# Mamba-2 part of a hybrid decoder layer on one core: activations pinned in line, a Ln as bias of the decays' exponents, three small steps moved from ScalarE to VectorE

## The chip, the cores and the metric

The kernel runs on one core of a Trainium2 chip. The metric is the device time of one execution in microseconds (us), lower is better. Engines are named as in the profile: PE (TensorE: matmuls), PEld (its weight loads), DVE (VectorE), ACT (ScalarE), POOL (GpSimd), SP (SyncE, which here issues DMAs only).

## The reference

One decoder layer over 256 tokens of width 2048, float32: a token mixer (an HGRN2 branch and a Mamba-2 branch, each gated and projected, then an output projection), cross-attention into 256 memory tokens, a gated feed-forward layer, and a final norm. What matters here is the Mamba-2 branch, cut to its core:

```python
xbc = silu(causal_dwconv(xbc_raw, conv_w, conv_b))      # 4 taps, per channel
xs, bm, cm = split(xbc)                                 # 8 groups of 4 heads of 64; 8 x 128; 8 x 128
dt = softplus(dt_raw + dt_bias);  a = dt * -exp(a_log)
# per group: state-space scan over time with decays exp(cum[t] - cum[s]), t >= s
y = ssd_chunk_scan(xs * dt, a, bm, cm) + d_skip * xs
y = y * silu(z)
y = y * rsqrt(mean(y * y, per group) + eps) * norm_g
```

The kernel computes the scan of a group without chunks: scores `bm^T cm`, multiplied by the decays `exp(cum[t] - cum[s])` and the causal mask, times `xs * dt`.

## The kernel before, in words

**Weights.** All dense products run on PE in a split form: a float32 weight tile of 128x2048 is fetched by SP (`issue`, L147), cast to a rounded high part `hi` on ACT (L133, in two halves of 1024 columns) and its remainder `lo` is formed on DVE (L134). Five buffers each of `hi` and `lo` (WB = 5) hold halves; a cast of a further half waits until PE has finished with the half five before it. `weights()` hands the next tile to PE, and at that point every entry of `background` (generators, one per scan) is advanced by one step. `project` uses one weight tile (two halves, 16 matmuls with `hi`, 16 with `lo`); `project_tok` uses four tiles.

**Order.** The program is written in one order, and a scheduler lays out a fixed instruction list for each engine from it, in which an instruction may be placed earlier if what it needs is there. Matmuls issued within a step are pinned by `keep_in_program_order`: what is pinned keeps its order among all pinned instructions. Each engine runs its list strictly in order. A `tile_critical` block is laid out as one piece.

**The Mamba-2 stage.** For group g, `m2_project(g)` runs four projections; each is joined from PSUM (`join`: a copy on ACT, L266; an add on DVE, L267) and convolved: the tap at lag 0 with the bias on ACT (L714), three further taps on DVE (L717). For even g, `m2_gates` (L701) projects z for two groups. `m2_scan(g)` is a background generator with pauses counted in weight tiles:

- Silu of x (L727), of B and C (L728), and for even g of z (L730); x is turned through DRAM: a DVE transpose (L502), four POOL DMAs out (L505), one back (L733). Eight Relus (L738, L740) form the exponents of the decays in two tiles `e` (lm), and two Exps (L745, L746) make the decays. The first Exp stands in a `tile_critical` block behind an explicit load of the table set `natural_log_exp_and_others` (L744).
- Three tiles later: scores on PE (`misc<-sz`), masked to `a` on DVE (L754) and copied on ACT (L756), multiplied into `e` on DVE (L758, twice); x times dt into `bb` on DVE (L762, twice).
- One tile later: the scan's products on PE (`misc<-e,bb`), then D's skip (L777), and the result is turned (L782).
- Three tiles later: times z (L790), squares with sums (L794, ACT), rsqrt as Ln and Exp (L285, L286, ACT), scaling by it (L798, ACT), and turned again (L801).
- Four tiles later: `split_turned` (L512 scaling on ACT, L281 cast on ACT, L282 remainder on DVE) writes the branch's output in split form.

Group 0's scan is begun by a generator that the last of four gate-and-branch passes of the HGRN2 branch (L811, L822) advances; groups 1 to 7 are projected after that, with z for groups 2, 4 and 6 ahead of those groups.

Of the kernel before, what the change touches and what calls it, by code (L numbers as in the profile page):

```python
# [9 lines left out]
F32 = mybir.dt.float32  # L10
# [3 lines left out]
AF = mybir.ActivationFunctionType  # L14
ALU = mybir.AluOpType
# [4 lines left out]
P = 128  # L20
T = 256
# [20 lines left out]
B = 32  # L42
# [22 lines left out]
def hybrid_trunk(ctx, tc, xT, memT, par, cst, msk, w_k0, w_ka, w_va, w_hg, w_hv, w_hog, w_ghg, w_bhg, w_dt,  # L65
                 w_z, w_m2, w_gm2, w_bm2, w_out, w_q, w_o, w_up, w_dn, fin_g, outT):
    nc = tc.nc
    V, S, G, PE = nc.vector, nc.scalar, nc.gpsimd, nc.tensor
# [20 lines left out]
    for h in range(1, HEADS, 2):  # L89
        order += [w_hg[h - 1 + i // 2, i % 2] for i in range(4)]  # L90
        q = h // 4 + 1
# [224 lines left out]
    ones = cp.tile([P, P], F32, name="ones")  # L316
# [6 lines left out]
    def pc(name, i=0, n=1):  # L323
        o, _ = PCOLS[name]
        return par_t[:, o + i:o + i + n]
# [13 lines left out]
    with tc.tile_pool(name="st", bufs=1) as st:  # L339
# [35 lines left out]
        for kk in range(KD // 2):  # L375
            raw = st.tile([P, 2 * W], F32, name="raw0", bufs=4)
            if kk == 0:
                for k in range(2):
                    nc.sync.dma_start(out=mraw[:, k, :], in_=memT[:, k, :])
                    nc.sync.dma_start(out=raw[:, k * W:(k + 1) * W],  # L380
                                      in_=w_k0[kk, :, k * W:(k + 1) * W])
# [16 lines left out]
        for n in range(KD):  # L398
# [16 lines left out]
            if n >= 10:  # L415
                for k in range((n - 10) * KD // 6, (n - 9) * KD // 6):
                    u = st.tile([P, T], F32, name="u", bufs=2)
                    V.scalar_tensor_tensor(out=u, in0=xraw[:, k, :], scalar=pc("mix_g", k),
                                           in1=r_xb, op0=ALU.mult, op1=ALU.mult)
# [16 lines left out]
                        op0=ALU.mult, op1=ALU.add)  # L436
        V.tensor_scalar(out=lb[:, 2], in0=lb[:, 1], scalar1=1e-30, scalar2=2.0 ** 60,
                        op0=ALU.max, op1=ALU.mult)
# [8 lines left out]
    mp = mx.enter_context(tc.tile_pool(name="mp", bufs=1))  # L447
# [61 lines left out]
    def split_turned(dst, yc, g):  # L509

        y = mp.tile([P, T], F32, name="jt", bufs=2)
        S.activation(out=y.rearrange("p (g b t) -> p g b t", b=P // B, g=2),  # L512
                     in_=yc.rearrange("p (b g t) -> p g b t", b=P // B, g=2), func=AF.Copy, scale=g)
        split(dst, y)
# [128 lines left out]
    for h in range(HEADS):  # L643
        background.append(hg_scan(h, *hg_project(h), vs[h // 4], sgs[h // 4]))
        if h % 2 and h // 4 + 1 == HEADS // 4:

            c = h % 4 // 2
# [56 lines left out]
    def m2_project(g):  # L704
        sz = mp.tile([P, 4, T], F32, name="sz", bufs=2)
        cb = mp.tile([P, 4, T], F32, name="vc", bufs=2)
        nc.sync.dma_start(out=cb, in_=cum_d[4 * g:4 * g + 4, :].partition_broadcast(P))
        for i in range(4):
            c = m2_chunk(g, i)
            ps = project(s2)  # L710
            raw = mp.tile([P, T], F32, name="t", bufs=1)
            join(mp, ps, raw)
            o = sz[:, i, :]
            S.activation(out=o, in_=raw, func=AF.Identity, bias=pc("m2_cb", c),  # L714
                         scale=pc("m2_cw", 4 * c + 3))
            for s in range(1, 4):
                V.scalar_tensor_tensor(out=o[:, s:T], in0=raw[:, 0:T - s],  # L717
                                       scalar=pc("m2_cw", 4 * c + 3 - s), in1=o[:, s:T],
                                       op0=ALU.mult, op1=ALU.add)
        return sz, cb  # L720

    def m2_scan(g, sz, cb, zt):
# [1 line left out]

        xc = mp.tile([P, 2 * T], F32, name="w", bufs=1)
        xv = xc.rearrange("p (m i t) -> p i m t", i=2, t=B)
        S.activation(out=xv, in_=sz[:, 0:2, :].rearrange("p i (m t) -> p i m t", t=B), func=AF.Silu)  # L727
        S.activation(out=sz[:, 2:4, :], in_=sz[:, 2:4, :], func=AF.Silu)  # L728
        if g % 2 == 0:
            S.activation(out=zt, in_=zt, func=AF.Silu)  # L730
        yd = turned(xc, T // B, "x_d")
        x = mp.tile([P, 2, T], F32, name="kq", bufs=2)
        G.dma_start(out=x, in_=yd.rearrange("(q p) c -> p q c", p=P))  # L733
        lm = [mp.tile([P, 2, 3 * P], F32, name=f"e{j}", bufs=1) for j in range(2)]
        for j in range(4):
# [3 lines left out]
                         bias=cum_tok[:, 0, hd:hd + 1])  # L739
            S.activation(out=l[:, T:3 * P], in_=cb[:, j, P:T], func=AF.Relu, scale=-1.0,  # L740
                         bias=cum_tok[:, 1, hd:hd + 1])

        with tc.tile_critical():  # L743
            nc.scalar.preload_act_table_set("natural_log_exp_and_others")  # L744
            S.activation(out=lm[0], in_=lm[0], func=AF.Exp, scale=-1.0)  # L745
        S.activation(out=lm[1], in_=lm[1], func=AF.Exp, scale=-1.0)  # L746
        yield from pause(3)
        bm, cm = sz[:, 2, :], sz[:, 3, :]
        ps = pm_.tile([P, 512], F32, name="misc")
# [5 lines left out]
                        in1=free(tri, 0, [(0, 2), (1, P)]), op=ALU.mult)  # L755
# [5 lines left out]
        for q in range(2):  # L761
            V.tensor_tensor(out=xd[:, q, :].rearrange("p (i b c) -> p i b c", i=2, c=B),  # L762
                            in0=x[:, q, :].rearrange("p (b i c) -> p i b c", i=2, c=B),
                            in1=free(dt_tok, 64 * q + 8 * g, [(4, 2), (1, 4), (0, B)]), op=ALU.mult)
        yield True
        yp = pm_.tile([P, 512], F32, name="misc")
        for j in range(4):
            rows = slice(64 * (j % 2), 64 * (j % 2) + 64)
            o = (j // 2) * T
# [5 lines left out]
        yv = y.rearrange("p (m i t) -> p i m t", i=2, t=B)  # L775
        for i in range(2):
            V.scalar_tensor_tensor(out=yv[:, i], in0=xv[:, i], scalar=pc("m2_d", 2 * g + i),  # L777
                                   in1=yp[:, i * T:(i + 1) * T].rearrange("p (m t) -> p m t", t=B),
                                   op0=ALU.mult, op1=ALU.add)
# [6 lines left out]
        r = mp.tile([P, 4], F32, name="rt", bufs=2)  # L786
        z0 = g % 2 * T
        yv = y.rearrange("p (n q c) -> p q n c", q=2, c=B)
        for q in range(2):
            V.tensor_tensor(  # L790
                out=y.rearrange("p (i b q c) -> p q b i c", i=2, q=2, c=B)[:, q],
                in0=yt[:, q, :].rearrange("p (b i c) -> p b i c", i=2, c=B),
                in1=zt[:, q, z0:z0 + T].rearrange("p (b i c) -> p b i c", i=2, c=B), op=ALU.mult)
            S.activation(out=yt[:, q, :].rearrange("p (n c) -> p n c", c=B), in_=yv[:, q],  # L794
                         func=AF.Square, accum_out=r[:, q:q + 1])
        rsqrt(r[:, 2:4], r[:, 0:2], 1.0 / T, eps2_t)
        for q in range(2):
            S.activation(out=yv[:, q], in_=yv[:, q], func=AF.Copy, scale=r[:, 2 + q:3 + q])  # L798
        yd = turned(y, T // B, "x_d")
        yc = mp.tile([P, 2, T], F32, name="yc", bufs=2)  # L800
        G.dma_start(out=yc, in_=yd.rearrange("(i p) t -> p i t", p=P))  # L801
        yield from pause(4 if g + 1 < GROUPS else 3)
        for i in range(2):
            split_turned(ym[:, 2 * g + i, :], yc[:, i, :], pc("m2_g", 2 * g + i))


    def gate(name="sz"):
# [7 lines left out]
    zt = m2_gates()  # L815
# [317 lines left out]
    def then(ins):  # L1133
        tc.keep_in_program_order(ins)
# [145 lines left out]
```

## Time and profile before

| | |
|---|---|
| median of 3 runs | 2263.75 us (2261.18, 2263.75, 2266.68) |
| profiled execution | 2263.27 us, of which the span 2261.1 us |
| PE busy in the span | 2233.0 us (99%) |
| DVE, ACT busy | 1622.3 us (72%), 1388.9 us (61%) |
| mean granted clock of PE | 0.996 |

The page gives busy time per engine, slices of the span, the chain that ended last, and groups of instructions. A group's row holds its line, engine, operation, tiles out<-in, count, busy us and mean ns of one, and the idle time of the engine just before, with what ended most of it. In a timeline the columns are start us, us, engine, line, operation; a bracket holds the idle time before and its releaser. The Mamba-2 groups 1 to 7 lie at about 720 to 1030 us of the span; PE runs the projections of groups 4 and 5 from 830 to 883 us, z for group 6 to 907 us, and groups 6 and 7 to 965 us.

### The profile page before, as it was taken

Reading aid. Unit: us, or ns where it says so; the run is one execution under the profiler, and the core shown is the slowest. Engines: PE = TensorE matmul, PEld = TensorE weight load, DVE = VectorE, ACT = ScalarE, POOL = GpSimd, SP = SyncE. Lnnn points to the kernel's source line nnn. Section 1 sums busy time; section 2 is a strip of 40 time slices with the busy share of each in tenths; the row PEclk is TensorE's granted clock in tenths of the full one; section 3 lists DMA queues with packets and bytes.
Section 4 is the critical chain, followed back from the end, with each engine's and each line's share of the span. In section 5 each row is a group of like instructions: output and inputs, shape, how many; then the busy total and the mean of one; then the engine's idle time right before and its main releaser. Section 6 shows DMA issues by size and latency. Waiting matters only on the chain.

```text
span 2261.1 us, 33653 instructions
## 1 busy us (share of the span) xinstructions
PE 2233.0 (99%) x13012; PEld 1916.3 (85%) x13012; DVE 1622.3 (72%) x2602; ACT 1388.9 (61%) x2181; POOL 118.1 (5%) x209
## 2 busy tenths in 40 slices
PE   9999999999999999899999999999999999999998
PEld 8888888888888887778888888888888888888887
DVE  8868888886645777665567765677777777779787
ACT  7567677777645687875455654556555555555554
POOL 0000001100100222120000000000000000000000
PEclk9999999999999999999999999999999999999999
DMA  8655555556655666565565644576555555555554
GB/s 311 239 181 181 192 184 180 184 178 217 217 191 197 217 216 209 205 209 200 189 229 210 223 156 175 177 225 215 193 187 189 192 194 190 186 196 214 205 214 158
DMA packets 94495, 453.70 MB, mean 201 GB/s; under 512 B 27744, under 2 KB 32384, under 8 KB 45312
## 3 DMA queue, kind: packets, MB, share of 16 engines
q1 hardware_dynamic: 69600, 432.36, 53.9%
q0 software_dynamic: 7808, 16.79, 2.8%
q10 hardware_dynamic: 16928, 2.42, 0.6%
q8 instruction: 102, 1.67, 0.3%
q14 instruction: 57, 0.47, 0.1%
HBM read 436.81 MB, written 16.81 MB: 201 GB/s over the span
## 4 chain that ended last, share of the span: by engine, by line
PE 56%; ACT 1%; DVE 1%; issue 0%; ACTq 0%; DVEq 0%
PE proj L82 49%; PE misc L82 4%; PE lev L82 3%; DVE lo L134 0%; ACT hi L133 0%; PE lev L844 0%; DVE e L758 0%; ACT L285 0%; ACTq L743 0%; PE lev L924 0%; ACT bb L794 0%; ACT L727 0%; ACT L286 0%; ACT L728 0%; ACT sz L728 0%
## 5 line engine op out<-in xcount | busy, mean ns | idle before, releaser
L134 DVE TENSOR_TENSOR lo<-raw,hi 128x1024 fp32r<-128x1024 f32 x738 | 893.8, 1222 | 471.3 <-ACT hi L133 428.4
L133 ACT CAST hi<-raw 128x1024 fp32r<-128x1024 f32 x737 | 768.5, 1049 | 401.6 <-PE proj L82 374.3
L82 PE MATMUL proj<-s,hi 128*128 128x512 f32 x3440 | 810.7, 391 | 1.4 <-ACT hi L364 1.4
L82 PEld LDWEIGHTS proj<-s,hi 128*128 128x128 f32 x3440 | 638.0, 188 | 129.1 <-ACT hi L364 1.9
L82 PE MATMUL proj<-hi,s 128*128 128x512 f32 x2218 | 695.7, 390 | 1.1 <-ACT hi L133 1.1
L82 PEld LDWEIGHTS proj<-hi,s 128*128 128x128 f32 x2218 | 416.3, 188 | 88.3 <-ACT hi L133 1.7
L82 PEld LDWEIGHTS proj<-s,lo 128*128 128x128 f32 x3440 | 433.3, 192 | 21.4 <-DVE lo L134 5.8
L82 PE MATMUL proj<-s,lo 128*128 128x256 f32 x3440 | 441.1, 284 | 9.2 <-DVE lo L134 9.2
L82 PE MATMUL proj<-lo,s 128*128 128x512 f32 x1109 | 431.8, 389 | 0.8 <-DVE lo L134 0.8
L82 PEld LDWEIGHTS proj<-lo,s 128*128 128x128 f32 x1109 | 208.4, 188 | 43.2 <-DVE lo L134 1.1
L266 ACT COPY jt<-proj 128x256 f32<-128x256 f32 x167 | 61.7, 370 | 84.8 <-PE proj L82 84.7
L168 ACT CAST hi<-raw 128x1024 fp32r<-128x1024 f32 (+1 forms) x56 | 52.1, 944 | 57.0 <-DVE raw L177 30.0
L505 POOL DMA_DIRECT2D x_d<-yq x96 | 55.8, 587 | 314.6 <-DVE yq L502 311.5
L169 DVE TENSOR_TENSOR lo<-raw,hi 128x1024 fp32r<-128x1024 f32 (+1 forms) x56 | 60.4, 1087 | 6.6 <-ACT hi L168 6.0
L717 DVE SCALAR_TENSOR_TENSOR sz<-t,par_t,sz 128x255 f32<-128x255 f32 (+2 forms) x96 | 45.6, 475 | 17.1 <-ACT sz L714 16.1
L505 POOL DMA_DIRECT2D y_d<-yq x64 | 35.0, 553 | 393.6 <-DVE sm L607 286.4
L1011 DVE SCALAR_TENSOR_TENSOR gc<-g,par_t,gc 128x255 f32<-128x255 f32 x88 | 42.2, 480 | 2.0 <-ACT gc L1009 0.6
L82 PE MATMUL proj<-hi,ha 128*128 128x512 f32 x104 | 36.7, 389 | 0.0
L1014 ACT ACTIVATE gc<-gc 128x256 f32<-128x256 f32 x44 | 18.4, 417 | 29.8 <-DVE gc L1011 29.7
L548 DVE TENSOR_TENSOR e<-bb 128x256 f32<-128x256 f32 x96 | 34.9, 418 | 0.1
L561 DVE TENSOR_TENSOR e<-e,kq 128x256 f32<-128x256 f32 x96 | 34.9, 417 | 0.0
L1015 DVE TENSOR_TENSOR gc<-gc,r_f 128x256 f32<-128x256 f32 x44 | 18.7, 425 | 20.9 <-ACT gc L1014 20.9
(306 smaller groups left out, 1815.0 us busy)
## 6 DMA issues: line engine op xcount, KB each, us to landing
raw<-in_w_up SPq DMA_DIRECT2D x88, 1024.0 KB, 4.8
raw<-in_w_dn SPq DMA_DIRECT2D x44, 1024.0 KB, 4.8
raw<-in_w_hg SPq DMA_DIRECT2D x32, 1024.0 KB, 4.8
raw<-in_w_m SPq DMA_DIRECT2D x32, 1024.0 KB, 4.9
raw<-in_w_hv SPq DMA_DIRECT2D x16, 1024.0 KB, 4.9
raw<-in_w_hog SPq DMA_DIRECT2D x16, 1024.0 KB, 4.8
raw<-in_w_ghg SPq DMA_DIRECT2D x16, 1024.0 KB, 4.8
raw<-in_w_z SPq DMA_DIRECT2D x16, 1024.0 KB, 4.8
```

The source lines that it names most:

```text
L82: ins = PE.matmul(*args, **kwargs)
L133: S.copy(out=hi[:, c - a:d - a], in_=raw[:, c:d])
L134: V.tensor_tensor(out=lo[:, c - a:d - a], in0=raw[:, c:d], in1=hi[:, c - a:d - a].bitcast(F32), op=ALU.subtract)
L168: S.copy(out=hi[:, 0:d - c], in_=raw[:, c:d])
L169: V.tensor_tensor(out=lo[:, 0:d - c], in0=raw[:, c:d], in1=hi[:, 0:d - c].bitcast(F32), op=ALU.subtract)
L266: S.copy(out=tmp, in_=ps[:, T:2 * T])
L505: G.dma_start(out=yd.rearrange("(n i) (b f) -> b i n f", i=B, b=P // B)[b], in_=yq[b * B:(b + 1) * B, :].rearrange("i (n f) -> i n f", n=n))
L548: V.tensor_tensor(out=lev[hw].rearrange("p (n c i) -> p n c i", c=2, i=hw), in0=free(bb, 0, [(2 * hw, nb), (T + hw, 2), (1, hw)]), in1=fre ...
L561: V.tensor_tensor(out=ev, in0=ev, in1=free(kq, 0, [(2 * hw, nb), (T + hw, 2), (1, hw)]), op=ALU.mult)
L717: V.scalar_tensor_tensor(out=o[:, s:T], in0=raw[:, 0:T - s], scalar=pc("m2_cw", 4 * c + 3 - s), in1=o[:, s:T], op0=ALU.mult, op1=ALU.add)
L1011: V.scalar_tensor_tensor(out=gc[:, s:T], in0=g[:, 0:T - s], scalar=pc("f_cw", 3 * c + 2 - s), in1=gc[:, s:T], op0=ALU.mult, op1=ALU.add)
L1015: V.tensor_tensor(out=gc, in0=gc, in1=r_f, op=ALU.mult)
```

## The change

- The lag-0 tap of the convolution (L714) becomes a DVE `tensor_scalar` with a multiply and an add.
- The Silus of B and C and of z are pinned in program order (for group 0 that of x too), so that they are not placed ahead of pinned matmuls that were written before them. Behind them, pinned as well, stands a Ln of a column of ones (its value is 0), and its output is the bias of both Exps of the decays. The `tile_critical` block and the explicit table load are gone, so that the two Exps are ordinary instructions behind all Relus.
- The scaling by the norm (L798, ACT) becomes a DVE `tensor_scalar` (L803).
- `split_turned` in the scan is replaced: one ACT scaling that writes the rounded high part straight into the output tile (L813), and two DVE `scalar_tensor_tensor` of 128 columns for the remainder (L818) in place of a scaling, a cast and one remainder of 256 columns. The HGRN2 branch keeps `split_turned`.

```diff
-            S.activation(out=o, in_=raw, func=AF.Identity, bias=pc("m2_cb", c),
-                         scale=pc("m2_cw", 4 * c + 3))
+            V.tensor_scalar(out=o, in0=raw, scalar1=pc("m2_cw", 4 * c + 3), scalar2=pc("m2_cb", c),
+                            op0=ALU.mult, op1=ALU.add)
...
-        S.activation(out=xv, in_=sz[:, 0:2, :].rearrange("p i (m t) -> p i m t", t=B), func=AF.Silu)
-        S.activation(out=sz[:, 2:4, :], in_=sz[:, 2:4, :], func=AF.Silu)
+        then = tc.keep_in_program_order
+        ins = S.activation(out=xv, in_=sz[:, 0:2, :].rearrange("p i (m t) -> p i m t", t=B),
+                           func=AF.Silu)
+        if g == 0:
+            then(ins)
+        then(S.activation(out=sz[:, 2:4, :], in_=sz[:, 2:4, :], func=AF.Silu))
         if g % 2 == 0:
-            S.activation(out=zt, in_=zt, func=AF.Silu)
+            then(S.activation(out=zt, in_=zt, func=AF.Silu))
+        r = mp.tile([P, 4], F32, name="rt", bufs=2)
+        then(S.activation(out=r[:, 0:1], in_=ones[:, 0:1], func=AF.Ln))
...
-        with tc.tile_critical():
-            nc.scalar.preload_act_table_set("natural_log_exp_and_others")
-            S.activation(out=lm[0], in_=lm[0], func=AF.Exp, scale=-1.0)
-        S.activation(out=lm[1], in_=lm[1], func=AF.Exp, scale=-1.0)
+        for j in range(2):
+            S.activation(out=lm[j], in_=lm[j], func=AF.Exp, scale=-1.0, bias=r[:, 0:1])
...
-            S.activation(out=yv[:, q], in_=yv[:, q], func=AF.Copy, scale=r[:, 2 + q:3 + q])
+            V.tensor_scalar(out=yv[:, q], in0=yv[:, q], scalar1=r[:, 2 + q:3 + q], scalar2=None,
+                            op0=ALU.mult)
...
-            split_turned(ym[:, 2 * g + i, :], yc[:, i, :], pc("m2_g", 2 * g + i))
+            dst, gn = ym[:, 2 * g + i, :], pc("m2_g", 2 * g + i)
+            cv = yc[:, i, :].rearrange("p (b q t) -> p q b t", q=2, t=B)
+            S.activation(out=dst[:, 0:T].rearrange("p (q b t) -> p q b t", q=2, t=B), in_=cv,
+                         func=AF.Copy, scale=gn)
+            for q in range(2):
+                hi, lo = [dst[:, o + q * P:o + (q + 1) * P].rearrange("p (b t) -> p b t", t=B)
+                          for o in (0, T)]
+                V.scalar_tensor_tensor(out=lo, in0=cv[:, q], scalar=gn, in1=hi.bitcast(F32),
+                                       op0=ALU.mult, op1=ALU.subtract)
```

Line numbers after the change are a little higher: the Silus are L730, L734, L736, the Ln L738, the Relus L746 and L748, the Exps L751, the mask L759, the products L763 and L767, the z product L795, the squares L799.

The lists of PE, POOL and SP keep their order but for two places (the scan's products of group 6 stand three matmuls later in PE's list; one weight fetch and one broadcast on SP change places). On ACT and DVE the order changes as follows.

ACT, at the decays of group 6 (`e_9632` and `e_9633` are its two decay tiles; before):

```order
L512 ACTIVATE jt<-yc,par_t 128x256
L743 NO_OP
L746 ACT_TABLE_LOAD
L746 ACTIVATE e_9633<-e_9633 128x768
L1276 UNCONDITIONAL_BRANCH
L744 ACT_TABLE_LOAD
L745 ACTIVATE e_9632<-e_9632 128x768
L743 UNCONDITIONAL_BRANCH
L281 CAST s_7502<-jt 128x256
L728 ACT_TABLE_LOAD
L728 ACTIVATE sz<-sz 128x512
L133 CAST hi<-raw 128x1024
```

The same place after the change (`e_9618`, `e_9619`):

```order
L133 CAST hi<-raw 128x1024 x2
L734 ACTIVATE sz<-sz 128x512
L736 ACTIVATE sg<-sg 128x1024
L738 ACT_TABLE_LOAD
L738 ACTIVATE rt<-ones 128x1
L266 COPY jt<-proj 128x256
L751 ACT_TABLE_LOAD
L751 ACTIVATE e_9618<-e_9618,rt 128x768
L751 ACTIVATE e_9619<-e_9619,rt 128x768
L133 CAST hi<-raw 128x1024 x2
```

The block's entry (the NO_OP, which waits for DVE and PE) and its branches are gone, and Silu stands ahead of the Exps; a table load stands ahead of the Ln and another ahead of the first Exp.

ACT, at the norm of group 5, which runs while PE projects for group 7 (before):

```order
L794 ACTIVATE bb,rt<-kq 128x256 x2
L714 ACTIVATE sz<-t,par_t 128x256
L285 ACT_TABLE_LOAD
L285 ACTIVATE rt<-rt,eps_t 128x2
L133 CAST hi<-raw 128x1024
L286 ACT_TABLE_LOAD
L286 ACTIVATE rt<-rt 128x2
L266 COPY jt<-proj 128x256
L798 ACTIVATE kq<-kq,rt 128x8x32 x2
L756 COPY a_1178<-misc 128x128
```

The same place after the change:

```order
L799 ACTIVATE bb,rt<-kq 128x256 x2
L266 COPY jt<-proj 128x256
L285 ACT_TABLE_LOAD
L285 ACTIVATE rt<-rt,eps_t 128x2
L133 CAST hi<-raw 128x1024
L286 ACT_TABLE_LOAD
L286 ACTIVATE rt<-rt 128x2
L761 COPY a_1178<-misc 128x128
```

The copy L266 out of the third projection of group 7's stage moves from behind the rsqrt to ahead of it, and L714 and L798 have left ACT.

DVE, at the scores of group 6, the same stretch of time (before):

```order
L717 SCALAR_TENSOR_TENSOR sz<-t,par_t,sz 128x254
L762 TENSOR_TENSOR bb<-kq,dt_tok 128x256
L717 SCALAR_TENSOR_TENSOR sz<-t,par_t,sz 128x253
L754 TENSOR_TENSOR a_1178<-misc,cst_t 128x2x128
L134 TENSOR_TENSOR lo<-raw,hi 128x1024
L502 STREAM_TRANSPOSE yq<-kq 128x512
L267 TENSOR_TENSOR t<-proj,jt 128x256
L758 TENSOR_TENSOR e_9632<-e_9632,a_1178 128x768
L758 TENSOR_TENSOR e_9633<-e_9633,a_1178 128x768
```

The same place after the change:

```order
L759 TENSOR_TENSOR a_1178<-misc,cst_t 128x2x128
L267 TENSOR_TENSOR t<-proj,jt 128x256
L803 TENSOR_SCALAR kq<-kq,rt 128x8x32 x2
L714 TENSOR_SCALAR sz<-t,par_t 128x256
L502 STREAM_TRANSPOSE yq<-kq 128x512
L717 SCALAR_TENSOR_TENSOR sz<-t,par_t,sz 128x255
L763 TENSOR_TENSOR e_9618<-e_9618,a_1178 128x768
L717 SCALAR_TENSOR_TENSOR sz<-t,par_t,sz 128x254
L763 TENSOR_TENSOR e_9619<-e_9619,a_1178 128x768
L717 SCALAR_TENSOR_TENSOR sz<-t,par_t,sz 128x253
L767 TENSOR_TENSOR bb<-kq,dt_tok 128x256 x2
```

The norm's scaling L803 now stands on DVE ahead of the two products with the decays, and both products x times dt, which stood ahead of the mask, stand last.

## The prediction

> **What bounds the kernel now.** I read the page's first lines, then busy time by stretch, then who waited for whom in the one stretch where TensorE (PE) is not full, and then the timelines of PE and ScalarE (ACT) there. The page:
>
> ```profile
> span 2261.1 us, 33653 instructions
> PE 2233.0 (99%) x13012; PEld 1916.3 (85%) x13012; DVE 1622.3 (72%) x2602; ACT 1388.9 (61%) x2181; POOL 118.1 (5%) x209
> ```
>
> PE's list does not get shorter by this change, so only its 28 idle us, and what they cost in clock, can be won. Three stretches (busy us of each engine, then PE's granted clock) show where they lie:
>
> ```profile
> 0.00:750.00 750.00, 747.57 (x5168) 639.41 (x5169) 555.66 (x1059) 504.45 (x874) 56.62 (x108) 1.00 0.58 205
> 750.00:1010.00 260.00, 242.94 (x1287) 204.35 (x1286) 177.10 (x267) 200.69 (x318) 57.69 (x95) 0.98 0.62 207
> 1010.00:2261.00 1251.00, 1242.46 (x6561) 1072.54 (x6559) 889.55 (x1278) 683.73 (x990) 3.75 (x6) 1.00 0.56 197
> ```
>
> The Mamba-2 groups, 750 to 1010, hold 17.06 of them; the rest is the kernel's start and end, which the change does not touch. In this stretch the waits are (engine, line and what it waited for: total us, times, longest):
>
> ```profile
> DVE lo L134 <- ACT hi L133: 50.4, 31, 7.1
> PE proj L82 <- DVE lo L134: 9.9, 4, 3.7
> ACT L744 <- PE proj L82: 8.4, 2, 5.6
> PE misc L82 <- DVE e L758: 3.4, 7, 1.2
> PE misc L82 <- DVE bb L762: 2.4, 1, 2.4
> PE proj L82 <- ACT hi L133: 1.1, 1, 1.1
> ```
>
> PE's four rows make 16.8 us. Most is PE waiting for a weight's remainder `lo`, made by VectorE (DVE), and DVE in its turn waits 50.4 us for ACT's casts: ACT is late. PE's timeline at three of the stalls, with undisturbed runs of the same matmuls beside them, shows a second loss:
>
> ```profile
> 858.03 7.44 PE L82 MATMUL proj<-s,hi 128*128 128x512 f32 x32
> 870.99 1.22 PE L82 MATMUL proj<-s,lo 128*128 128x256 f32 x8 [2.65 <-DVE lo L134]
> 872.05 9.05 PE L82 MATMUL proj<-s,hi 128*128 128x512 f32 x32
> ...
> 945.31 2.07 PE L82 MATMUL proj<-s,lo 128*128 128x256 f32 x16
> 951.12 3.56 PE L82 MATMUL proj<-s,lo 128*128 128x256 f32 x16 [3.74 <-DVE lo L134]
> ...
> 958.19 0.81 PE L82 MATMUL misc<-sz 128*128 128x256 f32 x4
> ...
> 964.71 1.74 PE L82 MATMUL misc<-e,bb 128*64 128x256 f32 x16
> ...
> 995.35 3.07 PE L82 MATMUL misc<-e,bb 128*64 128x256 f32 x16 [2.44 <-DVE bb L762]
> ```
>
> After the stalls of 2.65, 3.74 and 2.44 us the same matmuls take 9.05 for 7.44, 3.56 for 2.07 and 3.07 for 1.74: 1.6 + 1.5 + 1.3 = 4.4 us at a lower granted clock (the stretch's 0.98). So at most 16.8 + 4.4 = 21.2 us are there. Why ACT is late is seen ahead of the 3.74 us stall:
>
> ```profile
> 936.23 1.03 ACT L133 CAST hi<-raw 128x1024 fp32r<-128x1024 f32 x1
> ...
> 940.54 1.28 ACT L746 ACT_TABLE_LOAD   x1
> ...
> 944.18 1.28 ACT L744 ACT_TABLE_LOAD   x1 [1.50 <-DMA raw<-in_w_gm]
> ...
> 946.64 1.28 ACT L728 ACT_TABLE_LOAD   x1
> ...
> 948.67 1.99 ACT L133 CAST hi<-raw 128x1024 fp32r<-128x1024 f32 x2
> ...
> 957.62 1.28 ACT L285 ACT_TABLE_LOAD   x1
> ...
> 961.47 0.20 ACT L286 ACTIVATE rt<-rt 128x2 f32<-128x2 f32 x1
> ```
>
> Between two casts lie 11.4 us with three table loads, small steps, and the wait at the entry of the critical block. PE eats a half weight in 8 x 0.23 (7.44/32) and 8 x 0.13 (2.07/16), 2.9 us, and with five buffers ACT can be four halves ahead, 11.6 us: such a gap uses the lead up.
>
> **The change, part by part.** Groups that give the durations (count | busy us, mean ns | idle before):
>
> ```profile
> L714 ACT ACTIVATE sz<-t,par_t 128x256 f32<-128x256 f32 x32 | 19.1, 597 | 14.6 <-DVE t L267 14.4
> L798 ACT ACTIVATE kq<-kq,rt 128x256 f32<-128x256 f32 x16 | 7.2, 500 | 0.0
> L512 ACT ACTIVATE jt<-yc,par_t 128x256 f32<-128x256 f32 x32 | 15.8, 506 | 7.5 <-DMA yc<-x_d 5.0 <-DVE cum_tok L691 2.5
> L281 ACT CAST s<-jt 128x256 fp32r<-128x256 f32 x32 | 12.5, 402 | 0.4
> L744 ACT ACT_TABLE_LOAD x8 | 10.3, 1283 | 18.1 <-PE proj L82 8.4 <-DMA raw<-in_w_m 2.4 <-DMA vc<-cum_d 2.3
> L266 ACT COPY jt<-proj 128x256 f32<-128x256 f32 x167 | 61.7, 370 | 84.8 <-PE proj L82 84.7
> L524 DVE TENSOR_SCALAR lf<-sz,lnl 128x256 f32<-128x256 f32 x16 | 5.6, 350 | 0.3
> L282 DVE TENSOR_TENSOR s<-jt,s 128x256 fp32r<-128x256 f32 x32 | 12.9, 418 | 9.2 <-ACT s L281 9.2
> L717 DVE SCALAR_TENSOR_TENSOR sz<-t,par_t,sz 128x255 f32<-128x255 f32 x32 | 15.2, 475 | 16.1 <-ACT sz L714 16.1
> L502 DVE STREAM_TRANSPOSE yq<-kq 128x512 f32<-128x512 f32 x16 | 11.2, 705 | 4.7 <-ACT kq L798 4.6
> L758 DVE TENSOR_TENSOR e<-e,a 128x768 f32<-128x768 f32 x16 | 15.0, 951 | 0.0
> L134 DVE TENSOR_TENSOR lo<-raw,hi 128x1024 fp32r<-128x1024 f32 x738 | 893.8, 1222 | 471.3 <-ACT hi L133 428.4
> L730 ACT ACTIVATE sg<-sg 128x1024 f32<-128x1024 f32 x4 | 4.2, 1062 | 0.0
> L745 ACT ACTIVATE e<-e 128x768 f32<-128x768 f32 x8 | 6.8, 846 | 0.1
> ```
>
> *Off ACT:* L714 (32 x 0.597 = 19.1 us), L798 (7.2), half of L281 (16 x 0.402 = 6.4): 33 us busy in all; and the 18.1 us that ACT stood idle at the entry of the eight blocks. *Onto ACT:* eight Ln of one column, at most 0.3 each (the gap from L285's load to L286, below, bounds it), 2.4 us. Table loads stay about as many: the Exps lose theirs at L744 and get one at L751, the Ln adds one, while Silu needs one per group where it often needed two.
>
> *Onto DVE:* 32 convolution taps and 16 norm scalings; DVE's scalar multiply-add of this size is in the trace as L524, 0.350: 48 x 0.35 = 16.8 us. The 32 remainders L818 of 128 columns replace 16 of L282 (0.418). No row has that form; it is bounded by 0.21 (half of L282) and 0.475 (all of L717, twice as wide), and I take 0.34, nearer to L717, whose operation it is: 10.9 - 6.7 = +4.2 (bounds 0 to 8.5). DVE gets some 21 us, three quarters of it inside 750:1010: 177 + 16 = 193 us of the 239 that PE needs there without stalls. None of it costs anything as long as DVE keeps ahead, and there it does by 46 us.
>
> *What goes.* Four stalls on `lo` or `hi` follow directly behind a critical block, or behind Silu loads next to it; the widest gap between casts in the new list holds Silu and z's Silu (at most 1.06 each), two loads, Ln 0.3, a copy 0.37 and two Exps of 0.85, 7.1 us, so that they should all go, 9.9 + 1.1, with 3.1 of the clock. The 2.44 us stall on `bb` comes behind the 5.6 us wait of ACT at the last block: gone, with 1.3. The 3.4 us on `e` are short waits in which DVE gets to the mask late because ACT's copies and scaling were late; they shrink, but not at all places.
>
> *What is late next.* At the scores of group 6, DVE's list now has the scaling of group 5's norm (L803) ahead of the products with the decays. L803 needs the rsqrt, and ACT's list now has a PE-bound copy ahead of it. Take the end of group 7's third projection as zero (958.19 in the timeline above): L266 0.37, then from L285's load to L286's end 961.67 - 957.62 = 4.05 with a cast between: 4.4. Then DVE: L803 0.70, L714 0.35, L502 0.71, L717 0.48, L763 0.95, L717 0.48, L763 0.95, L717 0.48, first L767 0.42 (as L282): 5.5, or 4.6 if each overlaps its neighbour by 0.1 (two casts take 1.99 above, one 1.03). `bb` is ready at 9.0 to 9.9; PE wants it at 964.71 - 958.19 = 6.5, plus three matmuls that now stand ahead, 7.2. Stall 1.8 to 2.7; I take 2.3, and half of the 1.3 us of clock that such a stall cost. At group 4 the same chain has two more `lo` (2.4), a mask and a join (0.42 each as L282), a tap L714 and one L717 on DVE, 4.1 more, or 3.5 with overlaps: 12.5 to 14.0 in all; PE has a z tile of 24 matmuls (5.6) to run as well and wants it at 6.5 + 5.6 = 12.1: 0.4 to 1.9, I take 1.0. For the rest I leave 0.5. Together 4.5 us.
>
> Each table load is 1.28 us in the rows, and nothing stands between it and the next instruction: load, Ln, cast and load together end 3.85 us after their start at 957.62, 2 x 1.28 + 1.29. The Trainium skill (ScalarE: Activation LUTs, What ACT_TABLE_LOAD costs) puts a switch at about 2.66 us, with a drain behind the load. By that the group 6 chain would be 2.8 us longer and the total 2250; the measured rows decide.
>
> The Trainium skill (SBUF — State Buffer, Who interferes with whom) says that VectorE in a two-port mode locks GpSimd out of their shared port pair, which holds up descriptors of DMAs that GpSimd issues. That speaks against this change: the 48 `tensor_scalar` are of the kind, and the turns go through POOL's queue. No row shows such a wait. 48 x 0.35 = 17 us are spread over 300; if each of seven turns lost 0.35 x 5 issues = 1.75 us with no slack, that would be 12 us, and 2259.
>
> *Sum* against the profiled execution: 2263.27 - 21.2 + 4.5 = 2246.6; the median of the runs is 0.5 higher, so 2247.
>
> **Rivals.**
>
> 1. *All stalls go.* If the rsqrt of group 5 is early enough, nothing is left: 2263.75 - 21.2 = 2242.5. One way to it: Ln loads a table set that serves Exp as well. The Trainium skill (ScalarE: Activation LUTs, Table sets: the hidden batching unit) says that Ln then Exp need one load. Against it, the list of the new kernel has a load at L738 and one at L751 for every group, and before, the chain above shows a load for L285 and another for L286. If it were so, the chain would lose 1.28 and the loads behind it too. 13%, of which 3% for this way.
> 2. *Chains on DVE are late everywhere.* If each of the seven places where PE takes `e` and `bb` stalls like group 6 but shorter, 1.2 us, with clock lost at two: 7 x 1.2 + 2.6 = 11, so 2254, up to 2259. For it: DVE gets 16 us, and several links (rsqrt, scaling, turn, join) alternate between ACT and DVE. 14%.
> 3. *The waits on DVE do not shrink*, and the time is the same. DVE's idle time in the stretch was 260 - 177 = 83 us. With 193 us of work it may wait 46 us at no cost, and at 62 to 71 us the gain is used up. Of the 83, those on L714 go by themselves (16.1 in the row of L717, over the whole kernel). 9%.
> 4. *Slower: DVE becomes the bound.* The same mechanism beyond: if the 50.4 us on casts stay, since ACT now waits for DVE's convolution and z products, and the seven rsqrt chains add 4.4 us each to DVE's waits (31 us), DVE needs 193 + 81 = 274 us for the stretch instead of 260: +14, 2278. It decides from 71 us of waits on. Against it: ACT loses 33 us of work and 18 of idling, and those were what held the casts. 7%.
>
> **How the numbers follow.** My forecast, 2247 (2243 to 2252), has 57%. About 0.2%, 4.5 us, is what a measurement of this kernel can tell from no change. Faster holds the forecast and rivals 1 and 2: 84%; the same, rival 3, 9%; slower 7%. The range reaches from just under rival 1 to the upper end of rival 2: 2240 to 2258.
>
> **What would show it right or wrong.** In the profile after: PE's waits for `lo` and `hi` in the Mamba-2 groups under 1 us in total; a wait on `bb` of about 2 us once, at group 6; granted clock 0.99 or more there; DVE busier than ACT in that stretch; no ACT wait ahead of the decays' Exps. If PE still waits for `lo` by several us behind DVE rather than ACT, rivals 3 or 4 hold, and the step that failed is that DVE keeps ahead. If `bb` or `e` stalls appear at all groups, it is rival 2.

## The result, and the profile after

| | before | after |
|---|---|---|
| median | 2263.64 us (4 runs, 2261.18 to 2266.68) | 2251.39 us (4 runs, 2250.36 to 2252.09) |
| profiled execution, its span | 2263.27 us, 2261.1 us | 2251.54 us, 2249.4 us |
| PE idle in the span | 28.1 us | 19.7 us |

The changed kernel is faster by 12.3 us: ratio 0.9945, 95% interval 0.9928 to 0.9962. The forecast was 2247 us (2240 to 2258); 2251.39 lies in the range, 4.4 us above the value, and near the upper end of the narrower 2243 to 2252. The page of after:

```profile
span 2249.4 us, 33539 instructions
PE 2229.7 (99%) x13012; PEld 1913.8 (85%) x13012; DVE 1641.5 (73%) x2666; ACT 1363.6 (61%) x2123; POOL 118.1 (5%) x209
```

PE's busy time fell by 3.3 us with the same 13012 matmuls, which is granted clock, and its idle time by 8.4; together they are the 11.7 us by which the span is shorter. The stretch of the Mamba-2 groups, first as busy times (PE, PEld, DVE, ACT, POOL, then PE's clock), then as waits (total us, times, longest):

```profile
750.00:1010.00 260.00, 252.05 (x1341) 212.57 (x1340) 197.19 (x326) 194.72 (x296) 58.41 (x96) 0.99 0.66 219
```

```profile
DVE lo L134 <- ACT hi L133: 36.1, 25, 3.5
DVE kq L803 <- ACT rt L286: 8.4, 5, 2.3
PE misc L82 <- DVE bb L767: 6.4, 3, 4.5
PE misc L82 <- DVE e L763: 1.5, 1, 1.5
```

No row has PE waiting for `lo` or `hi`: the 11.0 us of before are gone. What is left are 7.9 us on the scan's operands `bb` and `e`, where before had 5.8. PE's timeline shows them at groups 2, 4 and 6; the row at 946.23 is the start of group 6's scores:

```profile
812.25 1.52 PE L82 MATMUL misc<-e,bb 128*64 128x128 f32 x14 [0.61 <-DVE bb L767]
...
867.93 7.44 PE L82 MATMUL proj<-s,hi 128*128 128x512 f32 x32
...
884.94 0.65 PE L82 MATMUL misc<-e,bb 128*64 128x256 f32 x2 [1.52 <-DVE e L763]
886.90 1.52 PE L82 MATMUL misc<-e,bb 128*64 128x128 f32 x14 [1.32 <-DVE bb L767]
...
946.23 0.81 PE L82 MATMUL misc<-sz 128*128 128x256 f32 x4
...
957.81 3.17 PE L82 MATMUL misc<-e,bb 128*64 128x256 f32 x16 [4.50 <-DVE bb L767]
```

Group 4 loses 2.8 us and group 6 loses 4.5, and the 16 matmuls behind the last stall take 3.17 us where 1.74 is what they took undisturbed: 1.4 us of clock. The costs of the moved steps, as groups (count | busy us, mean ns | idle before):

```profile
L751 ACT ACT_TABLE_LOAD x8 | 10.3, 1283 | 0.1
L714 DVE TENSOR_SCALAR sz<-t,par_t 128x256 f32<-128x256 f32 x32 | 13.0, 406 | 0.4
L738 ACT ACT_TABLE_LOAD x8 | 10.3, 1283 | 0.1
L818 DVE SCALAR_TENSOR_TENSOR s<-yc,par_t,s 128x128 fp32r<-128x128 f32 x32 | 9.2, 344 | 4.2 <-ACT s L813 4.2
L803 DVE TENSOR_SCALAR kq<-kq,rt 128x256 f32<-128x256 f32 x16 | 4.9, 351 | 8.9 <-ACT rt L286 8.9
```

The Exps' load now stands behind 0.1 us of idle time where it stood behind 18.1, and the Ln has a load of its own in every group. Now the chain at group 6 on ACT, from the Silu of B and C to the norm's Exp:

```profile
935.46 0.64 ACT L734 ACTIVATE sz<-sz 128x512 f32<-128x512 f32 x1 [0.91 <-DVE sz L717]
936.00 1.05 ACT L736 ACTIVATE sg<-sg 128x1024 f32<-128x1024 f32 x1
937.05 1.28 ACT L738 ACT_TABLE_LOAD   x1
938.35 0.20 ACT L738 ACTIVATE rt<-ones 128x1 f32<-128x1 f32 x1
...
938.83 1.28 ACT L751 ACT_TABLE_LOAD   x1
940.12 1.76 ACT L751 ACTIVATE e<-e,rt 128x768 f32<-128x768 f32 x2
941.79 1.98 ACT L133 CAST hi<-raw 128x1024 fp32r<-128x1024 f32 x2
...
947.38 0.42 ACT L799 ACTIVATE bb<-kq 128x256 f32<-128x256 f32 x1 [1.44 <-DVE kq L795]
...
948.52 0.35 ACT L266 COPY jt<-proj 128x256 f32<-128x256 f32 x1
948.89 1.28 ACT L285 ACT_TABLE_LOAD   x1
...
951.44 1.28 ACT L286 ACT_TABLE_LOAD   x1
952.73 0.20 ACT L286 ACTIVATE rt<-rt 128x2 f32<-128x2 f32 x1
```

And DVE over the same time:

```profile
942.86 2.36 DVE L134 TENSOR_TENSOR lo<-raw,hi 128x1024 fp32r<-128x1024 f32 x2 [1.58 <-ACT hi L133]
...
946.92 0.42 DVE L795 TENSOR_TENSOR kq<-bb,sg 128x256 f32<-128x256 f32 x1
...
952.97 0.62 DVE L803 TENSOR_SCALAR kq<-kq,rt 128x256 f32<-128x256 f32 x2 [2.31 <-ACT rt L286]
...
957.33 0.76 DVE L767 TENSOR_TENSOR bb<-kq,dt_tok 128x256 f32<-128x256 f32 x2
```

Read it backwards. PE takes `bb` at 957.81. DVE made it behind the scaling L803, for which it stood 2.31 us until ACT's Exp was through. ACT came to that Ln and Exp late, because the squares L799 waited for the product with z, L795; in DVE's list L795 stands behind three `lo`, a join and a tap, with no pause between them from 942.86 on. There DVE had stood 1.58 us for the cast that ACT began at 941.79, behind the Exps, the Ln and their loads. So the copy L266 stood at 948.52, 2.3 us after PE's third projection had ended (946.23).

### The profile page after: what moved, and what is told of

Same layout as the page of the kernel before. It is cut to its first block, busy times and chain, and to the rows that moved or that the text cites. A ratio compares the mean times of both kernels' runs of the same rounds, so it can differ in the third digit from the quotient of the medians.

```text
span 2249.4 us, 33539 instructions
## 1 busy us (share of the span) xinstructions
PE 2229.7 (99%) x13012; PEld 1913.8 (85%) x13012; DVE 1641.5 (73%) x2666; ACT 1363.6 (61%) x2123; POOL 118.1 (5%) x209
## 4 chain that ended last, share of the span: by engine, by line
PE 95%; DVE 2%; ACT 2%; issue 1%; DMA 0%; SPq 0%; DVEq 0%
PE proj L82 86%; PE misc L82 5%; PE lev L82 4%; DVE lo L134 0%; DVE sz L717 0%; DMA raw<-in_w_k 0%; ACT hi L133 0%; ACT e L751 0%; DVE e L763 0%; ACT L285 0%; ACT L751 0%; ACT L738 0%; PE lev L859 0%; DVE sz L714 0%; DVE t L267 0%
## 5 line engine op out<-in xcount | busy, mean ns | idle before, releaser
L82 PEld LDWEIGHTS proj<-s,lo 128*128 128x128 f32 x3440 | 431.7, 191 | 11.7 <-ACT s L281 0.5
L266 ACT COPY jt<-proj 128x256 f32<-128x256 f32 x167 | 61.9, 371 | 92.0 <-PE proj L82 92.0
```

Source lines behind the costliest of these rows:

```text
L82: ins = PE.matmul(*args, **kwargs)
L266: S.copy(out=tmp, in_=ps[:, T:2 * T])
```

## The experiments

Three questions: which part of the change brought the gain, what holds the rest, and whether the 21.2 us that were worked out as the most there can be are really there. Each was run beside the kernel before; ratios are to it, with 95% intervals. The medians of before were 2264.68, 2264.61, 2263.52 and 2263.59 us in the four sets of runs. Up to 1.2 us lie between them for one and the same kernel, so a difference of that size between kernels of two sets says nothing.

### Which part: the order on ACT or the work moved off it

*act_side*: before, with the tap, the scaling and `split_turned` left on ACT, and this alone (`...` marks lines of the change that are left out here):

```diff
+        then(S.activation(out=sz[:, 2:4, :], in_=sz[:, 2:4, :], func=AF.Silu))
...
+        then(S.activation(out=r[:, 0:1], in_=ones[:, 0:1], func=AF.Ln))
...
-        with tc.tile_critical():
-            nc.scalar.preload_act_table_set("natural_log_exp_and_others")
-            S.activation(out=lm[0], in_=lm[0], func=AF.Exp, scale=-1.0)
...
+            S.activation(out=lm[j], in_=lm[j], func=AF.Exp, scale=-1.0, bias=r[:, 0:1])
```

> The kernel before with only the ordering half of the change: no critical block, Silus pinned, Ln as bias of the Exps; the tap, the norm's scaling and the split of the turned rows stay on ScalarE. Theory A (the blocks and the table loads next to them made ScalarE late): the four waits for lo and the one for hi go, 2251 to 2255 us. Rival B (33 us too much work on ScalarE made it late): PE keeps waiting for lo, some 8 us in total, and the time is 2258 to 2263 us.

Measured: 2251.76 us, 0.9944 (0.9932 to 0.9957), as much as the whole change. PE waits for no `lo`; its waits on `e` are small and many, eight at groups 2 to 5, of which one at group 5:

```profile
923.04 0.88 PE L82 MATMUL misc<-e,bb 128*64 128x256 f32 x8 [1.40 <-DVE e L763]
```

*dve_side*: before, with the moves alone, the block left in (behind the last line stand the one ScalarE and two VectorE instructions of the change):

```diff
-            S.activation(out=o, in_=raw, func=AF.Identity, bias=pc("m2_cb", c),
-                         scale=pc("m2_cw", 4 * c + 3))
+            V.tensor_scalar(out=o, in0=raw, scalar1=pc("m2_cw", 4 * c + 3), scalar2=pc("m2_cb", c),
+                            op0=ALU.mult, op1=ALU.add)
...
-            S.activation(out=yv[:, q], in_=yv[:, q], func=AF.Copy, scale=r[:, 2 + q:3 + q])
+            V.tensor_scalar(out=yv[:, q], in0=yv[:, q], scalar1=r[:, 2 + q:3 + q], scalar2=None,
+                            op0=ALU.mult)
...
-            split_turned(ym[:, 2 * g + i, :], yc[:, i, :], pc("m2_g", 2 * g + i))
```

> The kernel before with only the moved work: tap, norm's scaling and remainders of the turned rows on VectorE; the critical blocks and unpinned Silus stay. Theory A: the blocks still hold ScalarE, the waits for lo stay above 6 us, 2257 to 2263 us. Rival B: without the 33 us ScalarE keeps ahead, 2250 to 2255 us.

Measured: 2262.49 us, 0.999 (0.9981 to 0.9999). Its waits in 750 to 1010:

```profile
ACT L744 <- PE proj L82: 16.1, 3, 5.9
PE misc L82 <- DVE e L758: 6.7, 7, 2.9
PE proj L82 <- DVE lo L134: 4.7, 4, 2.9
```

The waits for `lo` are 4.7 us where the theory had over 6, but they stay, and with 3.8 us on `bb` PE waits 15.2 us in all, where before had 16.8. With 28 us less to do (ACT 1360.7 us busy, before 1388.9), ACT stood longer at the block's entry: 16.1 us for PE where it was 8.4, and 26.5 us with its waits for DMAs there, where it was 16.2. Rival B falls: with the block in place, ACT was late through where it stood, not through how much it had to do.

*block_gone* and *pinned_block* take the order apart: the first is before with the block replaced by two plain Exps and nothing else, the second before with the Silus pinned and the block kept.

```diff
-        with tc.tile_critical():
-            nc.scalar.preload_act_table_set("natural_log_exp_and_others")
-            S.activation(out=lm[0], in_=lm[0], func=AF.Exp, scale=-1.0)
-        S.activation(out=lm[1], in_=lm[1], func=AF.Exp, scale=-1.0)
+        for j in range(2):
+            S.activation(out=lm[j], in_=lm[j], func=AF.Exp, scale=-1.0)
```

> The kernel before with one edit: the critical block and its explicit load go, the two Exps stand as plain instructions; no pinned Silu, no Ln. Theory A1 (the block itself, its entry wait and its place in the list, made ScalarE late): 2250 to 2254 us, waits for lo under 1 us. Rival A2 (what counts is that Silus and Exps no longer alternate, which the pins and the Ln bring): Exps float between the Silus, table loads stay, 2256 to 2262 us.

> The kernel before with only the Silus pinned in line; the critical block stays, no Ln. Theory A1: the block's entry still makes ScalarE stand, 2256 to 2262 us with waits for lo of some us. Rival A2: 2250 to 2255 us.

Measured: block_gone 2247.61 us, 0.993 (0.9917 to 0.9944), below the range that its theory gave, though its waits for `lo` are 1.7 us where the theory had under 1:

```profile
DVE lo L134 <- ACT hi L133: 49.2, 36, 6.1
...
PE proj L82 <- DVE lo L134: 1.7, 2, 1.2
```

pinned_block took 2262.07 us, 0.9992 (0.9983 to 1.0001), 0.1 above the range of A1. In it ACT stands 14.0 us at the block's entry, all for DMAs, and PE waits 11.0 us on `e` and 3.3 on `lo`.

So the block is the cause, A1. Without it ACT has as much to do (1391.8 us busy, before 1388.9) and loads tables as often (56 loads, before 54), and yet PE's waits in the stretch are 5.3 us for 16.8. The explicit load and the place of the Exps in the list went with the block; no run parts the three. Taking the block out alone is worth more, 17.0 us, than the change with all its parts, 12.3. That was not expected by any theory here: something in the change costs what its other parts bring.

### What holds the rest: the norm's chain, and the Ln

*norm_after* takes the scaling of groups 3 and 5 (`ins` below) out of DVE's way:

```diff
         rsqrt(r[:, 2:4], r[:, 0:2], 1.0 / T, eps2_t)
+        if g in (3, 5):
+            yield from pause(2)
...
+            if g in (3, 5):
+                then(ins)
...
-        yield from pause(4 if g + 1 < GROUPS else 3)
+        yield from pause({3: 2, 5: 2, GROUPS - 1: 3}.get(g, 4))
```

> The changed kernel, but the norm's scaling of groups 3 and 5 is pinned two weight tiles later, so that VectorE's list has the products with the decays and x times dt of groups 4 and 6 ahead of it. Theory C (the residual 8 us of PE's waits come from VectorE standing at that scaling until ScalarE's Ln and Exp are through): the waits of 2.8 us at group 4 and 4.5 us at group 6 go, with 1.5 us of clock, 2242 to 2245 us. Rival D (VectorE has too much to do there whatever the order): the waits stay above 4 us, 2248 us or more.

Measured: 2248.57 us, 0.9932 (0.992 to 0.9945): the time of rival D, though not for its reason. PE's wait at group 6 fell from 4.50 to 2.08 us and at group 4 from 2.8 to 1.4, and one of 2.22 came up at group 5, where DVE stands 2.44 us at the scaling of group 4, which this edit leaves in its place. At group 6 DVE no longer stands at the scaling, and what it stands for instead is the mask's copy L761:

```profile
952.07 0.96 DVE L763 TENSOR_TENSOR e<-e,a 128x768 f32<-128x768 f32 x1 [1.65 <-ACT a L761]
```

```profile
949.17 1.28 ACT L286 ACT_TABLE_LOAD   x1
...
951.77 0.27 ACT L761 COPY a<-misc 128x128 f32<-128x128 f32 x1
```

L761 stands behind Ln and Exp (and a copy and a cast) in ACT's list. The order on DVE was one part of the matter; the chain on ACT is the other.

*sqrt_rec* shortens that chain. It computes the reciprocal root in another way:

```diff
-        rsqrt(r[:, 2:4], r[:, 0:2], 1.0 / T, eps2_t)
+        S.activation(out=r[:, 2:4], in_=r[:, 0:2], func=AF.Sqrt, bias=eps2_t, scale=1.0 / T)
+        V.reciprocal(out=r[:, 2:4], in_=r[:, 2:4])
```

> The changed kernel, but the norm's reciprocal root is made as a Sqrt on ScalarE and a reciprocal of two columns on VectorE, in place of Ln and Exp: one table load in the chain for two, and no cast between. Theory C: the chain is 2.3 us shorter at both places, so the wait at group 6 falls from 4.5 to about 2.2 us, that at group 4 from 2.8 to about 0.5, and the time is 2245 to 2248 us. Rival D: the list on VectorE is as long, nothing moves, 2250 to 2252 us.

Measured: 2247.02 us (2242.95 to 2247.93), 0.9925 (0.9911 to 0.9938). In its profiled execution, the one of 2242.95, the wait at group 6 is 1.79 us, group 4 has 0.32 and group 7 0.40. ACT's chain there is one load of 1.28 us and a Sqrt of 0.30. The median lies in the range of theory C.

*sqrt_after* has both edits.

> The changed kernel with both edits: the norm's reciprocal root as Sqrt on ScalarE and a reciprocal on VectorE, and the scaling of groups 3 and 5 pinned two weight tiles later. Theory C, with the share that showed on ScalarE (the mask's copy stands behind Ln and Exp there): nearly no wait on e and bb is left, 2242 to 2245 us. Rival F (with the short root the scaling's place no longer counts): as with the short root alone, 2246 to 2248 us.

Measured: 2243.51 us (2240.18 to 2245.98), 0.991 (0.9896 to 0.9923), in the range of theory C. At groups 4 and 6 one wait of 0.23 us is left. But a new one stands at group 7, where norm_after has none and sqrt_rec 0.40:

```profile
984.53 3.13 PE L82 MATMUL misc<-e,bb 128*64 128x256 f32 x16 [2.58 <-DVE rt L802]
```

```profile
983.95 0.43 DVE L767 TENSOR_TENSOR bb<-kq,dt_tok 128x256 f32<-128x256 f32 x1 [3.91 <-DMA kq<-x_d]
```

The wait is put down to the reciprocal L802; ahead of that DVE had stood 3.91 us for the DMA that brings the turned x. Why that came late was not followed. That both edits are needed is not separated from one alone, since the intervals overlap.

*no_ln* drops the Ln and the bias, *copy_bias* keeps the dependence without the load:

```diff
-        r = mp.tile([P, 4], F32, name="rt", bufs=2)
-        then(S.activation(out=r[:, 0:1], in_=ones[:, 0:1], func=AF.Ln))
...
-            S.activation(out=lm[j], in_=lm[j], func=AF.Exp, scale=-1.0, bias=r[:, 0:1])
+            S.activation(out=lm[j], in_=lm[j], func=AF.Exp, scale=-1.0)
```

```diff
-        then(S.activation(out=r[:, 0:1], in_=ones[:, 0:1], func=AF.Ln))
+        then(S.activation(out=r[:, 0:1], in_=ones[:, 0:1], func=AF.Copy, scale=0.0))
```

> The changed kernel without the Ln and its bias; Silus stay pinned. Seven table loads of 1.28 us fewer on ScalarE. Theory C (only the chain through the norm's Ln and Exp costs time now, and these loads do not lie in it): 2249 to 2252 us. Rival E (ScalarE's load still counts): 2244 to 2248 us. Rival A2 (the Ln holds the Exps behind the Silus and is needed for that): waits for lo come back, 2254 us or more.

> The changed kernel with the Ln of the ones made a Copy with scale zero (its value is 0 as well): the Exps still wait behind the Silus, but the table load ahead of the Ln goes, 8 x 1.28 us on ScalarE. Theory E (that load, in ScalarE's list ahead of the squares of the norm, is what makes the chain at groups 4 and 6 late): 2244 to 2247 us, as without the Ln. Rival O (what costs is that the Exps stand behind the Silus, where they would otherwise fill ScalarE's wait for the convolution): 2249 to 2252 us.

Measured: no_ln 2243.99 us, 0.9913 (0.9899 to 0.9926); copy_bias 2247.34 us (2244.91 to 2248.36), 0.9929 (0.9917 to 0.9941). Theory C missed for no_ln, by 5 us, and rival E's time came out: the loads do count, because they stand in ACT's list ahead of the squares with which the chain begins. Of the 7.4 us that the Ln costs, some 4.1 go with its load and some 3.3 with the order that it forces; copy_bias lies between no_ln and the changed kernel and its interval reaches into both, so that split is rough. The 2247.34 us of copy_bias lie 0.3 above the range that theory E gave it. That the order counts beside the loads shows in their number too: no_ln has 45 table loads and copy_bias 44, and no_ln is the faster. ACT at group 6 in no_ln shows the order:

```profile
928.66 1.28 ACT L749 ACT_TABLE_LOAD   x1
929.95 1.58 ACT L749 ACTIVATE e<-e 128x768 f32<-128x768 f32 x2
931.54 1.28 ACT L734 ACT_TABLE_LOAD   x1
932.83 0.63 ACT L734 ACTIVATE sz<-sz 128x512 f32<-128x512 f32 x1
...
941.43 0.42 ACT L797 ACTIVATE bb<-kq 128x256 f32<-128x256 f32 x1 [1.75 <-DVE kq L793]
```

```profile
943.19 0.81 PE L82 MATMUL misc<-sz 128*128 128x256 f32 x4
...
952.28 0.65 PE L82 MATMUL misc<-e,bb 128*64 128x256 f32 x2 [1.55 <-DVE bb L765]
```

The Exps now stand ahead of the Silu of B and C, which in the changed kernel waited 0.91 us for the convolution with the Exps held behind it. The squares start 1.76 us before PE's projection ends; in the changed kernel they start 1.15 us behind it, and PE's wait is 1.55 us for 4.50. In copy_bias the same squares and PE's wait:

```profile
942.96 0.42 ACT L799 ACTIVATE bb<-kq 128x256 f32<-128x256 f32 x1 [0.34 <-DVE kq L795]
```

```profile
943.18 0.81 PE L82 MATMUL misc<-sz 128*128 128x256 f32 x4
...
953.40 1.85 PE L82 MATMUL misc<-e,bb 128*64 128x256 f32 x16 [3.14 <-DVE bb L767]
```

0.22 us ahead: 1.37 earlier than in the changed kernel, about the one load of 1.28, and the wait is shorter by 1.36.

### What is there at most

*gone_moves* is dve_side with the two plain Exps of block_gone: the change without its pins and its Ln. *sqrt_noln* is no_ln with the short root, *gone_sqrt* gone_moves with it. Beside the moves, gone_moves has the first two lines, gone_sqrt all of:

```diff
+        for j in range(2):
+            S.activation(out=lm[j], in_=lm[j], func=AF.Exp, scale=-1.0)
...
+        S.activation(out=r[:, 2:4], in_=r[:, 0:2], func=AF.Sqrt, bias=eps2_t, scale=1.0 / T)
+        V.reciprocal(out=r[:, 2:4], in_=r[:, 2:4])
```

> The kernel before without the critical block (plain Exps, no pins, no Ln) and with the three steps moved to VectorE: the changed kernel without pins and Ln. Against the block's removal alone (2247.6) it shows what the moves are worth once the block is gone; against the changed kernel without its Ln (2244.0) what the pins are worth. Theory G (the moves relieve ScalarE, which is late again at places): 2243 to 2245 us. Rival H (the moves are worth nothing, the pins bring the 3.6 us): 2246.5 to 2249 us.

> The changed kernel without the Ln and its bias, and with the norm's reciprocal root as Sqrt on ScalarE and a reciprocal on VectorE. Theory C: the waits left without the Ln (0.83 us at group 4, 1.55 at group 6) hang on the same chain and go: 2241 to 2243.5 us. Rival I (the two cures overlap wholly, the rest is elsewhere): 2243.5 to 2245 us.

> The kernel before without the critical block, with the three moved steps, no pins and no Ln, and with the norm's reciprocal root as Sqrt on ScalarE and a reciprocal on VectorE. Theory J (PE's idle time in the Mamba-2 groups is used up, as without Ln and with the short root, where PE waited for nothing there): no gain over that kernel's 2241.3, 2240.5 to 2242 us. Rival K (the pins cost something by themselves): below 2240 us.

Measured: gone_moves 2242.43 us, 0.9907 (0.9894 to 0.9921); sqrt_noln 2241.28 us, 0.9905 (0.989 to 0.992); gone_sqrt 2239.89 us (2239.74 to 2240.5), 0.9893 (0.9877 to 0.991), the fastest, 23.7 us below before. sqrt_noln lies in the range of theory C. Theory G holds in direction (its range began 0.6 higher): with the block gone, the moves bring 5.2 us over block_gone, though with the block in place they brought 2.2; the two intervals overlap by a little. The pins show no gain: gone_moves without them is not above no_ln with them. Whether they cost something stays open: gone_sqrt is 0.1 us below the bound that rival K was given, and 1.4 to 1.6 us lie between kernels with and without pins, in different sets and with overlapping intervals. PE in gone_sqrt, in the same stretch:

```profile
750.00:1010.00 260.00, 260.00 (x1391) 220.38 (x1390) 205.22 (x340) 185.93 (x277) 61.07 (x101) 1.00 0.69 228
```

260.00 busy us of 260, at full clock. There is nothing left to win here but PE's own work.

## Why the prediction was right, and where it was not

- *The bound and the cause.* That at most 21.2 us in this stretch can be won was nearly right. The best kernel, where PE does not wait in the stretch at all, gains 23.7 us by medians and 22.8 between profiled executions (2263.27 to 2240.50). Of the 1.6 us by which 22.8 exceeds the bound, 1.3 are clock: PE's busy time falls by 5.7 us in gone_sqrt (2233.0 to 2227.3) where the three quoted places gave 4.4. That ACT's lateness came from the critical block is shown by block_gone, and that it was not ACT's amount of work by dve_side. One sign of it was misread: the 50.4 us that DVE waits for casts were taken to say that ACT is late. In block_gone DVE still waits 49.2 us for them, and PE 1.7 us for `lo`. Whether ACT is late for PE shows in PE's waits alone.
- *What goes.* The waits on `lo` and `hi`, and that on `bb` at group 7, went as forecast. In the sum that was 11.0 + 3.1 and 2.4 + 1.3. The stretch's clock is 0.99, DVE is busier there than ACT (197.19 and 194.72 us; 193 was forecast for DVE), and no wait stands ahead of the decays' Exps: these signs held. The sign of one wait on `bb` of about 2 us, at group 6 only, did not: there are three, 6.4 us in all.
- *What is late next: the term that was mis-sized.* The chain was forecast at group 6 with a stall of 2.3 us and at group 4 with 1.0; they measured 4.5 and 2.8, and the sum of 4.5 us should have been some 9 (7.9 of waits and 1.4 of clock). The length of the chain was right: from L266's start to the first `bb` 957.75 - 948.52 = 9.2 us at group 6 (the first L767 of two, 957.33 + 0.42; 9.0 to 9.9 forecast), and 886.85 - 873.82 = 13.0 at group 4 (12.5 to 14.0), by these rows of ACT and DVE:

```profile
873.82 0.35 ACT L266 COPY jt<-proj 128x256 f32<-128x256 f32 x1
```

```profile
886.44 0.41 DVE L767 TENSOR_TENSOR bb<-kq,dt_tok 128x256 f32<-128x256 f32 x1
```

Wrong was its start, "Take the end of group 7's third projection as zero": L266 stood 2.3 us behind it, and at group 4 2.2 behind the middle of the row at 867.93 (871.65, the end of the third projection). 2.3 + 2.3 and 1.0 + 2.2 give the measured stalls within 0.4. What starts the chain is not PE but ACT's squares, behind DVE's product with z, behind DVE's `lo`, behind ACT's Exps, Ln and loads (at group 4 DVE stands 2.79 us for the cast behind the Exps).
- *The step that made it so.* "Onto ACT: eight Ln of one column, at most 0.3 each" priced the Ln at 2.4 us of ACT's time and at nothing for PE. The list of the new kernel showed its load at L738; its place ahead of the chain was not followed. Dropping the Ln gave 7.4 us, through its load and through the order that it forces.
- *The rivals.* Rival 1, all stalls gone at 2242.5, did not happen in the changed kernel. gone_moves has its time (2242.43) with 1.3 us of waits left; sqrt_noln and gone_sqrt, where PE waits for nothing in the stretch, are below it. The way to this rival that was named, one table set for Ln and Exp, does not happen: L738 and L751 have eight loads each in after. The Trainium skill (ScalarE: Activation LUTs, Table sets: the hidden batching unit) has Ln then Exp under one load; the list here places two, and the measurement decides. Rival 2, late chains at all places, is seen in act_side, where ACT still does the scaling: eight waits on `e` of 0.29 to 1.41 us at groups 2 to 5, with group 6 at 1.9 + 1.5. The moves took these away and put them into the two chains instead. Rivals 3 and 4 needed DVE to fall behind with `lo`; it did not. Their budget for DVE's waits, with the gain used up at 62 to 71 us, did not hold: in after DVE is idle for 62.8 of the stretch's 260 us, and the gain is there.
- *The moved steps.* Estimated 0.35, 0.35 and 0.34 us, measured 0.406, 0.351 and 0.344: 1.8 us more for the tap, which DVE had to spare. No price of 12 us for `tensor_scalar` beside POOL's turns shows: the moves gain 5.2 us once the block is gone. A smaller price is not excluded.

The one term accounts for the miss: losses of 9.3 us for 4.5 are 4.8 more, and the measured median lies 4.4 above the forecast.

## What to carry to other kernels

A block that the scheduler must lay out as one piece made its engine stand at the entry here, and of the work taken off that engine a good part came back as standing time; take such a block out first and price the moves afterwards. An instruction that is there only to order others cost what its table load and the order it forces cost on the path, not its own 0.2 us. For a chain across engines, find out what starts it by following the list backwards from its first instruction on each engine; a length that is right from a wrong start gives a stall that is wrong by the whole shift.

## What the runs showed of the hardware

The clock lost behind a stall does not follow from its length. 16 matmuls took 3.17 us behind 4.50 us of waiting in after, 3.56 behind 2.08 in norm_after, but 1.85 behind 3.14 in copy_bias. The granted clock was 0.50 from 957.8 to 961.0, 0.54 from 954.9 to 958.6 and 1.00 from 953.4 to 955.3. The row of norm_after:

```profile
954.94 3.56 PE L82 MATMUL misc<-e,bb 128*64 128x256 f32 x16 [2.08 <-DVE bb L767]
```

The Trainium skill (TensorE: Matmul & The Clock Gate, Part 1) has the clock gate watch a free-running window, so that the moment at which the clock is released depends on where in the window the first matmul lands. These three rows fit that in so far as the length alone does not decide; the windows themselves are not seen in any run here.

The runs of sqrt_rec, with a stall of 1.79 us left in its profile, spread over 5.0 us (2242.95 to 2247.93), those of gone_sqrt, which never waits in the stretch, over 0.8. The mean granted clock goes with it: 0.999 in the fastest run of sqrt_rec and 0.997 in the slowest, and 0.999 in all four of gone_sqrt. An estimate from these, 0.2% of 2245 us, is 4.5 us, so most of the spread is likely clock; what makes it fall differently from run to run no experiment separated.
